# MLP weight blocks prepared a block further ahead, and DVE passes put in another order

## The chip, the cores and the metric

The kernel runs on one core of a Trainium2 chip. The metric is the device time of one execution in microseconds, the median of three runs. Five engines work beside each other, each through its own queue in order: PE (TensorE, the matmuls), DVE (VectorE) and ACT (ScalarE) for elementwise work, POOL (GpSimd) and SP (SyncE), which here mostly issue DMAs.

## What is computed

One layer of a hybrid decoder on 544 token columns (512 prompt, 32 sample tokens), in fp32:

```python
def decoder_layer(x, caches, norm_mix, w_in, ..., w_out, norm_ffn, w_up, w_down, rel_bias):
    h = rms_norm(x, norm_mix)
    z = h @ w_in                      # 2048 -> 5632: q, k, v of 3 x 4 heads, u and g of the gMLP
    ...                               # dilated window attention, and u * (W_s g + b) in chunks
    x = x + jnp.concatenate([attn, gm], axis=-1) @ w_out
    h2 = rms_norm(x, norm_ffn)
    x = x + jnp.square(jax.nn.relu(h2 @ w_up)) @ w_down      # 2048 -> 8192 -> 2048
    return x, new_kv, g
```

## The kernel before

The order on each engine is the order of the Python statements (`manual_schedule`), so what stands earlier in the code of an engine's queue holds up what stands later. The tile framework adds the semaphore waits: between SBUF accesses by the slice that they touch, for a PSUM tile by the whole tile, and for a buffer of a pool when its earlier tile is done with.

**Precision.** An fp32 factor is split into a high part (a cast to fp32r by ACT) and the remainder (a subtraction by DVE), and each product is three matmuls: high by high, high by low, low by high.

**Before the MLP.** The input projection (88 tiles), attention and gMLP come first; a planner (`Plan`) deals their small steps out between the projection's weight tiles. `gate_mix(f)` (L590) makes the four spatial gate products in the PSUM tiles `po`, `ms`, `po`, `ms`; `gate_add(f)` (L595) reads them on DVE, one planner slot later. The output projection makes 16 row tiles in pairs (`M_ORDER`); for each, `residual` (L662) adds the input on DVE, squares on ACT and stores to `x1d` from POOL's queue, and `terms(k)` (L694) makes of a pair the seven terms of the MLP's input, which `run(1)` casts to `th[k]` (ACT) and `run(2)` subtracts to `tl[k]` (DVE). `run(0)` adds the squares into `ssq`. The last pair of tiles is computed in halves: both first halves, then both second halves.

**The MLP.** It uses a seven-product scheme for 2x2 block matrices: the seven products `qs[1..7]` stand in PSUM, products 1 and 2 in one tile (`pa`), 6 and 7 in another (`pb`), 5, 4 and 3 in a tile each. There are 64 stages, 32 for `w_up` and 32 for `w_down`, of four units each; unit u = 4 s + g. A unit uses one weight block of 512 KB (`load`, from SP's queue, three slots `raw`) and is 42 matmuls in the order 1, 2, 6, 7, 5, 4, 3. For a block `prepare` (L739) does: ACT casts `vh` of the raw quarters (L751); DVE makes four opening sums `vs` (L752, two at once; L754; L755); ACT casts these (L756); DVE subtracts for `vl` (L757 from the raw quarters, L758 from the sums). `vs`, `vh` and `vl` have two buffers.

In the queues, unit u has: the fetch of block u + 3, `prepare` of block u + 1, the hooks put down for (s, g), the matmuls of unit u, and after the fourth unit `combine` (L789): ACT copies product 1 to `w` (L791), DVE forms four sums of the seven products (L792 to L798). After an up stage these are squared relu (`square`, hook at the next stage's unit 1), get the three sums of `sums` (L682; unit 2) and are stored to `rd[p]` from POOL's queue. In a down stage pair k's terms are replaced by those of the next stage: `load_terms` (L861) brings `rd` to `tl[k]`, `down_terms` (L868) casts to `th[k]` on ACT (L871) and subtracts on DVE (L872), one pair each stage, and eight pairs while up passes to down. `down_out` (L887) adds to `yd` in DRAM; the last eight stages scale and store `y` (`scaled`, L874). `start_sum` (L836) scales the residual into `yd` during the up stages, and `scale_back` (L809) makes the norm's factors in stages 2 to 4. Pair 7's terms are made by `last_terms` (L766), a hook of unit (0, 1).

## Time and profile before

| | us |
|---|---|
| median of the runs shown | 2180.43 (2175.71 to 2183.02) |
| the profiled execution | 2178.95, span 2177.2 |
| first matmul of the MLP | 765.88 |
| first matmul of its down stages | 1453.58 |
| mean granted TensorE clock | 0.988 |

The span goes from the first to the last instruction. The MLP's matmuls, 10752 of 16392, take up the last two thirds of it. Matmul records overlap (a matmul's record lasts 0.29 us, where the next starts 0.125 later), so starts tell more than lengths. An idle time in brackets behind a row is the time that the engine stood before this instruction, with the instruction whose end released it.

### The profile page before, as it was taken

Reading aid. Unit: us, or ns where it says so; the run is one execution under the profiler, and the core shown is the slowest. Engines: PE = TensorE matmul, PEld = TensorE weight load, DVE = VectorE, ACT = ScalarE, POOL = GpSimd, SP = SyncE. Lnnn points to the kernel's source line nnn. Section 1 sums busy time; section 2 is a strip of 40 time slices with the busy share of each in tenths; the row PEclk is TensorE's granted clock in tenths of the full one; section 3 lists DMA queues with packets and bytes.
Section 4 is the critical chain, followed back from the end, with each engine's and each line's share of the span. In section 5 each row is a group of like instructions: output and inputs, shape, how many; then the busy total and the mean of one; then the engine's idle time right before and its main releaser. Section 6 shows DMA issues by size and latency. Waiting matters only on the chain.

```text
span 2177.2 us, 40916 instructions
## 1 busy us (share of the span) xinstructions
PE 2091.0 (96%) x16392; PEld 2060.1 (95%) x16392; DVE 1754.4 (81%) x3566; ACT 929.3 (43%) x1296; POOL 235.4 (11%) x534
## 2 busy tenths in 40 slices
PE   8989999999889989999999999988999999999998
PEld 8989989899889989999999999988999999999998
DVE  5355767566677889989999998889888888898987
ACT  5324243342543444444444544454444444444442
POOL 3121120211211100000000000010000000000101
PEclk9999999999999999999999999999999999999999
DMA  5365655656564534445555444474565656564665
GB/s 191 99 187 174 213 200 183 205 175 206 184 190 151 181 116 133 164 157 181 170 174 178 168 162 143 151 281 151 159 179 157 182 154 181 155 182 154 217 204 156
DMA packets 109695, 378.13 MB, mean 174 GB/s; under 512 B 12640, under 2 KB 12752, under 8 KB 109504
## 3 DMA queue, kind: packets, MB, share of 16 engines
q1 hardware_dynamic: 81744, 243.58, 34.3%
q0 software_dynamic: 27760, 131.94, 19.9%
q8 instruction: 128, 2.10, 0.4%
q14 instruction: 63, 0.52, 0.1%
HBM read 305.87 MB, written 69.21 MB: 172 GB/s over the span
## 4 chain that ended last, share of the span: by engine, by line
PE 46%; issue 33%; DMA 9%; DVE 7%; POOL 2%; ACT 2%; POOLq 0%; SPq 0%; DVEq 0%; ACTq 0%
PE pt L87 13%; PE pt L931 6%; PE pt L933 6%; PE pt L932 6%; DMA kv<-in_kc_dram 3%; PE sm L931 2%; PE sm L932 2%; PE po L931 2%; PE po L932 2%; PE sm L933 2%; PE ms L931 2%; PE ms L933 2%; PE po L933 2%; PE ms L932 2%; DMA kv<-in_vc_dram 1%
## 5 line engine op out<-in xcount | busy, mean ns | idle before, releaser
L931 PE MATMUL pt<-th,vh 128*128 128x272 f32 x2048 | 597.9, 292 | 23.7 <-DVE o L792 16.6
L932 PE MATMUL pt<-tl,vh 128*128 128x272 f32 x2048 | 594.7, 290 | 7.3 <-DVE tl L872 7.3
L933 PE MATMUL pt<-th,vl 128*128 128x272 f32 x2048 | 594.0, 290 | 3.8 <-DVE vl L757 3.8
L756 ACT CAST vh<-vs 128x1024 fp32r<-128x1024 f32 x256 | 269.4, 1052 | 405.4 <-DVE vs L755 403.9
L931 PEld LDWEIGHTS pt<-th,vh 128*128 128x128 f32 x2048 | 388.6, 190 | 30.8 <-DVE o L792 20.7
L932 PEld LDWEIGHTS pt<-tl,vh 128*128 128x128 f32 x2048 | 389.3, 190 | 8.4 <-DVE tl L872 8.4
L933 PEld LDWEIGHTS pt<-th,vl 128*128 128x128 f32 x2048 | 389.7, 190 | 4.2 <-DVE vl L757 4.2
L751 ACT CAST vh<-raw 128x768 fp32r<-128x768 f32 x256 | 213.5, 834 | 339.3 <-PE po L932 202.8
L758 DVE TENSOR_TENSOR vl<-vs,vh 128x1024 fp32r<-128x1024 f32 x256 | 313.8, 1226 | 54.3 <-ACT vh L756 53.7
L87 PE MATMUL pt<-hh,wh 128*128 128x272 f32 x1408 | 302.8, 297 | 6.0 <-DVE wh L78 6.0
L87 PE MATMUL pt<-hl,wh 128*128 128x272 f32 x1408 | 294.5, 291 | 0.5 <-DVE hl L183 0.5
L87 PE MATMUL pt<-hh,wl 128*128 128x272 f32 x1408 | 294.5, 291 | 0.0
L757 DVE TENSOR_TENSOR vl<-raw,vh 128x768 fp32r<-128x768 f32 x256 | 244.0, 953 | 19.3 <-ACT vh L751 17.6
L87 PEld LDWEIGHTS pt<-hh,wh 128*128 128x128 f32 x1408 | 224.1, 192 | 17.0 <-ACT hh L182 6.0
L79 DVE TENSOR_TENSOR wl<-raw,wh 128x512 fp32r<-128x512 f32 x208 | 145.3, 700 | 108.0 <-ACT wh L78 107.0
L87 PEld LDWEIGHTS pt<-hl,wh 128*128 128x128 f32 x1408 | 225.0, 192 | 0.9 <-DVE hl L183 0.9
L87 PEld LDWEIGHTS pt<-hh,wl 128*128 128x128 f32 x1408 | 223.8, 192 | 0.0
L78 ACT CAST wh<-raw 128x512 fp32r<-128x512 f32 x200 | 121.5, 615 | 151.3 <-PE pt L87 137.2
L752 DVE TENSOR_TENSOR vs<-raw 128x512 f32<-128x512 f32 x256 | 175.1, 684 | 0.0
L931 PE MATMUL po<-th,vh 128*128 128x272 f32 x512 | 147.8, 289 | 0.0
L931 PE MATMUL sm<-th,vh 128*128 128x272 f32 x512 | 147.5, 288 | 0.0
L933 PE MATMUL po<-th,vl 128*128 128x272 f32 x512 | 147.5, 288 | 0.0
(233 smaller groups left out, 3768.5 us busy)
## 6 DMA issues: line engine op xcount, KB each, us to landing
raw<-in_w_up_dram SPq DMA_DIRECT2D x128, 512.0 KB
raw<-in_w_down_dram SPq DMA_DIRECT2D x128, 512.0 KB
raw<-in_w_in_dram SPq DMA_DIRECT2D x84, 512.0 KB
tl<-rd POOLq DMA_DIRECT2D x39, 952.0 KB, 7.7
rd<-f POOLq DMA_DIRECT2D x32, 952.0 KB, 4.4
kv<-in_kc_dram SPq DMA_DIRECT2D x96, 256.0 KB
kv<-in_vc_dram SPq DMA_DIRECT2D x96, 256.0 KB
yd<-o POOLq DMA_DIRECT2D x39, 544.0 KB, 5.5
```

What stands on the lines that cost most here:

```text
L78: copy(wh, r)
L79: V.tensor_tensor(wl, r, wh.bitcast(F32), op=OP.subtract)
L87: mm(pt[:, c, :NH], wt[:, j, :], at[:, c * NH:(c + 1) * NH], start=start and n == 0, stop=stop and n == 2)
L751: A.copy(vh[:, :3 * VB], raw[:, VB:])
L752: V.tensor_tensor(pair(vs[:, :2 * VB]), raw[:, None, :VB].to_broadcast([P, 2, VB]), pair(raw[:, VB:3 * VB]), op=OP.add)
L756: A.copy(vh[:, 3 * VB:], vs)
L757: V.tensor_tensor(vl[:, :3 * VB], raw[:, VB:], vh[:, :3 * VB].bitcast(F32), op=OP.subtract)
L758: V.tensor_tensor(vl[:, 3 * VB:], vs, vh[:, 3 * VB:].bitcast(F32), op=OP.subtract)
L931: mm(qs[n], vh[:, c], th[k][:, t, :], start=first, stop=False)
L932: mm(qs[n], vh[:, c], tl[k][:, t, :], start=False, stop=False)
L933: mm(qs[n], vl[:, c], th[k][:, t, :], start=False, stop=last)
```

## The change

- `prepare` is cut in two. `sum_weights` makes the opening sums, now two blocks ahead: L752 and L754 ahead of the split of the next block, L755 behind it. `split_weights` does both casts (ACT) and both subtractions (DVE), one block ahead.
- `combine` uses three slices of one tile `w` (one buffer; two before) and another order of its sums.
- Where output projection and MLP meet, block 0 is summed and split ahead of the last two residuals, and block 1 summed behind them. What `run(2)` and `run(0)` do for pair 6 and the last squares moves to hooks of units (0, 0) and (0, 1).
- The three sums after an up stage go to units 2, 3 and 0 of the next stages, the store to `rd` with the last one. `start_sum`'s scaling goes from unit 3 to unit 1. From the ninth pair on `down_terms` goes from unit 2 or 3 of the load's stage to unit 1 of the next one.
- Gate products 2 and 3 go to tiles of the small PSUM ring (two buffers) instead of `po` and `ms`.

The matmuls, their order, the loads and the arithmetic stay.

```diff
     def gate_mix(f):
-        po = gates[f]["po"] = ps.tile([P, 512], F32, name=("po", "ms")[f % 2])
+        po = gates[f]["po"] = ps.tile([P, 512], F32, name=("po", "ms")[f]) if f < 2 else small_psum()
...
     def sums(f):
         V.tensor_tensor(f[:, 0:2, :], f[:, 7:8, :].to_broadcast([P, 2, NH]), f[:, 4:7:2, :], op=OP.subtract)
+        yield
         V.tensor_tensor(f[:, 2, :], f[:, 6, :], f[:, 0, :], op=OP.subtract)
+        yield
         V.tensor_tensor(f[:, 3, :], f[:, 5, :], f[:, 2, :], op=OP.subtract)
...
-    run(0)
+    pts = [main_psum() for _ in range(2)]
+    for part in range(2):
+        for pt in pts:
+            half(pt, part)
     mix.close()
...
-        A.copy(vh[:, :3 * VB], raw[:, VB:])
+    def sum_weights(u):
+        raw = raws[u]
+        vs = summed[u] = uw.tile([P, 4 * VB], F32, name="vs", tag=f"vs{u % 2}")
         V.tensor_tensor(pair(vs[:, :2 * VB]), raw[:, None, :VB].to_broadcast([P, 2, VB]), pair(raw[:, VB:3 * VB]),
                         op=OP.add)
         V.tensor_tensor(part(vs, 2), part(vs, 1), part(raw, 1), op=OP.add)
+        yield
         V.tensor_tensor(part(vs, 3), part(vs, 2), part(raw, 3), op=OP.add)
+        yield
+
+    def split_weights(u):
+        raw, vs = raws[u], summed[u]
+        vh, vl = (uw.tile([P, 7 * VB], F32R, name=n, tag=f"{n}{u % 2}") for n in ("vh", "vl"))
+        A.copy(vh[:, :3 * VB], raw[:, VB:])
         A.copy(vh[:, 3 * VB:], vs)
         V.tensor_tensor(vl[:, :3 * VB], raw[:, VB:], vh[:, :3 * VB].bitcast(F32), op=OP.subtract)
         V.tensor_tensor(vl[:, 3 * VB:], vs, vh[:, 3 * VB:].bitcast(F32), op=OP.subtract)
...
     for i in range(3):
-        fetch(units[i])
-    ready = [prepare()]
+        fetch(i)
+    list(sum_weights(0))
+    split_weights(0)
+    for m, pt in zip(M_ORDER[KD - 2:], pts):
+        residual(m, pt)
+    list(sum_weights(1))
 
     def last_terms():
         nonlocal yp
+        run(0)
...
     def combine(c11, c12, c21, c22):
-        w = uw.tile([P, NH], F32, name="w", bufs=2)
-        A.copy(w, qs[1])
-        V.tensor_tensor(c11, qs[2], w, op=OP.add)
-        V.tensor_tensor(w, qs[6], w, op=OP.subtract)
-        V.tensor_tensor(c21, qs[7], w, op=OP.add)
-        V.tensor_tensor(w, qs[5], w, op=OP.add)
-        V.tensor_tensor(c22, qs[5], c21, op=OP.add)
-        V.tensor_tensor(c21, qs[4], c21, op=OP.add)
-        V.tensor_tensor(c12, qs[3], w, op=OP.subtract)
+        w = uw.tile([P, 3, NH], F32, name="w")
+        w1, w2, w3, x = (w[:, i, :] for i in (0, 1, 0, 2))
+        A.copy(w1, qs[1])
+        V.tensor_tensor(w2, qs[6], w1, op=OP.subtract)
+        V.tensor_tensor(c11, qs[2], w1, op=OP.add)
+        V.tensor_tensor(x, qs[7], w2, op=OP.add)
+        V.tensor_tensor(w3, qs[5], w2, op=OP.add)
+        V.tensor_tensor(c22, qs[5], x, op=OP.add)
+        V.tensor_tensor(c21, qs[4], x, op=OP.add)
+        V.tensor_tensor(c12, qs[3], w3, op=OP.subtract)
...
+    hook(0, 0, run, 2)
     hook(0, 1, last_terms)
...
-        hook(8 + 2 * q, 3, rest)
+        hook(8 + 2 * q, 1, rest)
...
+        parts = sums(f)
+        hook(p + 1, 1, square)
+        hook(p + 1, 2, partial(next, parts))
+        hook(p + 1, 3, partial(next, parts))
+
+        def last():
+            next(parts, None)
             G.dma_start(out=rd[p], in_=f[:, :7, :])
 
-        hook(p + 1, 1, square)
-        hook(p + 1, 2, rest)
+        hook(p + 2, 0, last)
...
-                                ((first, 0), (first, 2)), ((first, 0), (first, 2)), ((first, 1), (first, 3)))):
+                                ((first, 0), (first, 2)), ((first, 0), (first, 2)), ((first, 1), (first + 1, 1)))):
...
         hook(UPG + t, 1, load_terms, t + PAIRS)
-        hook(UPG + t, 2, down_terms, t + PAIRS)
+        hook(UPG + t + 1, 1, down_terms, t + PAIRS)
...
-        if u + 3 < len(units):
-            fetch(units[u + 3])
+        fetch(u + 3)
+        sums_next = sum_weights(u + 2) if u + 2 < len(units) else iter(())
+        next(sums_next, None)
         if u + 1 < len(units):
-            ready.append(prepare())
+            split_weights(u + 1)
+        next(sums_next, None)
         for fn in hooks.get((s, g), []):
             fn()
```

## Rows read from the trace of the kernel before

**Rows 1.** The page: busy us of each engine, share of the span, instructions.
```profile
PE 2091.0 (96%) x16392; PEld 2060.1 (95%) x16392; DVE 1754.4 (81%) x3566; ACT 929.3 (43%) x1296; POOL 235.4 (11%) x534
```

**Rows 2.** Stretches of the MLP: length, PE, PEld, DVE, ACT, POOL busy, PEclk, DMA.
```profile
765.88:793.34 27.46, 23.38 (x168) 22.72 (x168) 23.38 (x32) 10.60 (x12) 0.00 (x0) 0.94 0.29 89
793.34:923.00 129.66, 128.09 (x1013) 127.04 (x1013) 119.00 (x192) 58.79 (x67) 5.77 (x10) 1.00 0.46 152
923.00:1429.40 506.40, 506.40 (x4035) 506.40 (x4033) 457.49 (x729) 235.86 (x264) 21.24 (x40) 1.00 0.49 164
1453.58:1490.34 36.76, 27.51 (x168) 26.00 (x168) 33.24 (x37) 21.39 (x18) 1.06 (x2) 0.86 0.54 211
1490.34:2145.28 654.94, 640.19 (x5040) 635.12 (x5041) 580.75 (x846) 285.28 (x299) 49.26 (x71) 1.00 0.59 176
```

**Rows 3.** Who PE waited for in the MLP: us in total, times, longest us.
```profile
PE pt L931 <- DVE o L792: 16.6, 17, 2.0
```

**Rows 4.** DVE in one down stage, in time: start us, us, instruction, idle before.
```profile
1641.01 0.44 DVE L792 TENSOR_TENSOR o<-pt,w 128x272 f32<-128x272 f32 x1
1641.55 0.44 DVE L793 TENSOR_TENSOR w<-pt,w 128x272 f32<-128x272 f32 x1
...
1644.17 0.68 DVE L752 TENSOR_TENSOR vs<-raw 128x512 f32<-128x512 f32 x1
1644.89 0.43 DVE L754 TENSOR_TENSOR vs<-vs,raw 128x256 f32<-128x256 f32 x1
1645.35 0.43 DVE L755 TENSOR_TENSOR vs<-vs,raw 128x256 f32<-128x256 f32 x1
1645.69 0.95 DVE L757 TENSOR_TENSOR vl<-raw,vh 128x768 fp32r<-128x768 f32 x1
1646.89 1.23 DVE L758 TENSOR_TENSOR vl<-vs,vh 128x1024 fp32r<-128x1024 f32 x1 [0.25 <-ACT vh L756]
1648.03 0.69 DVE L752 TENSOR_TENSOR vs<-raw 128x512 f32<-128x512 f32 x1
...
1656.78 2.14 DVE L872 TENSOR_TENSOR tl<-tl,th 128x1904 fp32r<-128x1904 f32 x1 [0.92 <-ACT th L871]
...
1662.70 0.43 DVE L792 TENSOR_TENSOR o<-pt,w 128x272 f32<-128x272 f32 x1
```

**Rows 5.** DVE in the last stage, in time.
```profile
2155.37 1.28 DVE L876 TENSOR_TENSOR o<-o,rb 128x1088 f32<-128x1088 f32 x1
```

**Rows 6.** DVE where up passes to down, first and last of 36 rows.
```profile
1448.99 4.19 DVE L872 TENSOR_TENSOR tl<-tl,th 128x1904 fp32r<-128x1904 f32 x2 [0.46 <-ACT th L871]
...
1489.86 0.43 DVE L792 TENSOR_TENSOR o<-pt,w 128x272 f32<-128x272 f32 x1
```

**Rows 7.** PE in the MLP's first stage, in time: its first matmul and one of block 3.
```profile
765.88 0.39 PE L931 MATMUL pt<-th,vh 128*128 128x272 f32 x1 [2.28 <-ACT vh L751]
...
787.76 0.39 PE L933 MATMUL pt<-th,vl 128*128 128x272 f32 x1 [1.85 <-DVE vl L757]
```

**Rows 8.** DVE at the same place, in time.
```profile
763.64 0.72 DVE L664 TENSOR_TENSOR x<-pt,x 128x544 f32<-128x544 f32 x1 [0.24 <-PE pt L87]
...
775.94 0.96 DVE L757 TENSOR_TENSOR vl<-raw,vh 128x768 fp32r<-128x768 f32 x1 [0.84 <-ACT vh L751]
...
783.08 2.14 DVE L691 TENSOR_TENSOR tl<-f,th 128x1904 fp32r<-128x1904 f32 x1 [1.85 <-ACT th L691]
```

**Rows 9.** PE at the third gate product and the second output tile, in time.
```profile
653.42 2.05 PE L593 MATMUL po<-gwt,gt 128*128 128x128 f32 x8 [3.65 <-DVE z L598]
...
667.33 0.77 PE L87 MATMUL pt<-cat,wh 128*128 128x272 f32 x4
```

**Rows 10.** DVE between these two: the read of the last input tile.
```profile
663.83 0.72 DVE L630 TENSOR_TENSOR z<-pt,rb 128x544 f32<-128x544 f32 x1
```

**Rows 11.** The page: a group (busy us, mean ns, idle before) and a DMA issue.
```profile
L752 DVE TENSOR_TENSOR vs<-raw 128x512 f32<-128x512 f32 x256 | 175.1, 684 | 0.0
...
tl<-rd POOLq DMA_DIRECT2D x39, 952.0 KB, 7.7
```

More of the change, by code (lines that the diff above doesn't have):

```diff
@@ L2 @@
 from functools import partial
-from itertools import cycle, islice
+from itertools import islice
 import numpy as np
@@ L697, in terms @@
             V.scalar_tensor_tensor(dst, halves(x1[m]), gn[:, 16 + m:17 + m], halves(rb), op0=OP.mult, op1=OP.mult)
-        sums(f)
+        list(sums(f))
         after[1].append(partial(A.copy, th[k], f[:, :7, :]))
@@ L709, in half @@
         run(part)
-    for i, m in enumerate(M_ORDER):
-        if 2 <= i < KD - 2:
+    for i, m in enumerate(M_ORDER[:KD - 2]):
+        if i >= 2:
             pts = [main_psum()]
@@ L715, in hybrid_layer_kernel @@
                 half(pts[0], part)
-        elif i == KD - 2:
-            pts = [main_psum() for _ in range(2)]
-            for part in range(2):
-                for pt in pts:
-                    half(pt, part)
         residual(m, pts.pop(0))
@@ L724, in hybrid_layer_kernel, with fetch, part, pair @@
             after[0].append(first_scale)
-        for k in {3: [0], 4: [1]}.get(i, [i // 2] if i % 2 and 4 < i < KD - 1 else []):
+        for k in {3: [0], 4: [1]}.get(i, [i // 2] if i % 2 and i > 4 else []):
             terms(k)
-        if i + 2 < KD:
-            x_load(M_ORDER[i + 2])
-    run(0)
+        x_load(M_ORDER[i + 2])
+    pts = [main_psum() for _ in range(2)]
+    for part in range(2):
+        for pt in pts:
+            half(pt, part)
     mix.close()
     uw = ctx.enter_context(tc.tile_pool(name="uw", bufs=1, side="right", reuse_waits="tile"))
-    turns = cycle(range(2))
-    raws = []
-    def fetch(src):
-        raws.append(load(src))
-    def prepare():
-        raw = raws.pop(0).rearrange("p a b -> p (a b)")
-        n = next(turns)
-        vs = uw.tile([P, 4 * VB], F32, name="vs", tag=f"vs{n}")
-        vh, vl = (uw.tile([P, 7 * VB], F32R, name=v, tag=f"{v}{n}") for v in ("vh", "vl"))
-        def part(t, i):
-            return t[:, i * VB:(i + 1) * VB]
-        def pair(t):
-            return t.rearrange("p (a b) -> p a b", a=2)
-        A.copy(vh[:, :3 * VB], raw[:, VB:])
+    raws, summed, ready = {}, {}, {}
+    def fetch(u):
+        if u < len(units):
+            raws[u] = load(units[u]).rearrange("p a b -> p (a b)")
+    def part(t, i):
+        return t[:, i * VB:(i + 1) * VB]
+    def pair(t):
+        return t.rearrange("p (a b) -> p a b", a=2)
+    def sum_weights(u):
+        raw = raws[u]
+        vs = summed[u] = uw.tile([P, 4 * VB], F32, name="vs", tag=f"vs{u % 2}")
         V.tensor_tensor(pair(vs[:, :2 * VB]), raw[:, None, :VB].to_broadcast([P, 2, VB]), pair(raw[:, VB:3 * VB]),
@@ L852, in square @@
             A.activation(f[:, 4:, :], f[:, 4:, :], AF.Square)
-        def rest():
-            sums(f)
+        parts = sums(f)
[4 more added lines that the diff above has]
+            next(parts, None)
             G.dma_start(out=rd[p], in_=f[:, :7, :])
-        hook(p + 1, 1, square)
-        hook(p + 1, 2, rest)
+        hook(p + 2, 0, last)
     def load_terms(n):
```

4 lines of the change are left out of this document (2 added, 2 removed).

## Prediction

> **What bounds the kernel now.** I read the page first: TensorE (PE) is busy 96% of the span, VectorE (DVE) 81% [rows 1]. That does not say what a microsecond taken from DVE is worth, so the next view cuts the MLP into stretches [rows 2]. A stage is 168 matmuls. In the third stretch 24 stages take 506.40 us, or 21.10 each, with PE busy throughout: no stage can be shorter. Against that floor the other stretches lose:
>
> - the first stage 27.46 - 21.10 = 6.4 (and 2.3 before its first matmul);
> - the next six 129.66 - 126.6 = 3.1;
> - the last up stage, from 1429.40 to 1453.58, 3.1, and the first down stage 36.76 - 21.10 = 15.7, together 18.7;
> - the 30 down stages from 1490.34, 654.94 - 633.0 = 21.9.
>
> These 52 us are all that work on the MLP can win. The third view is who ends PE's waits: in the down stages it is L792, the first DVE instruction of `combine`, 17 times [rows 3]. The first matmul of a stage writes a PSUM tile that L792 has to have read. The fourth view tells why L792 is late [rows 4]: in this down stage DVE stands still only for ScalarE (ACT), and from L792 to the next L792 is 1662.70 - 1641.01 = 21.69 us, longer than PE's 21.10. So DVE sets the pace there, as it does in the first stage and where up passes to down; in between PE does.
>
> **The change part by part.**
>
> *One weight block on DVE.* Before, from L752 to the next L752 is 1648.03 - 1644.17 = 3.86 [rows 4]: starts 0.72, 0.46, 0.34, 1.20 and 1.14 apart. Two parts of that go. L755 reads what L754 has just written, and starts 0.46 after it; an instruction that touches nothing of its predecessor's starts 0.34 after one of that size (L755 to L757). I count 0.35. With L755 behind L758 this saves 0.11. L758 stands 0.25 for ACT's cast of the sums; once the sums lie a block ahead that cast follows the first one at once, so 1.20 becomes 0.95. The pair L752, L754 stays together, 0.72. New block: 0.72 + 0.35 + 0.95 + 1.14 + 0.35 = 3.51, saving 0.35.
>
> *`combine`.* Before 1644.17 - 1641.01 = 3.16 for seven instructions, of which one that overwrites its predecessor's operand starts 0.54 behind it (L792 to L793) [rows 4]. In the new order neighbours share no slice: 7 x 0.35 = 2.45, saving 0.71. Against it, the tile that the next stage's first matmul writes is now read by the second instruction, not the first: 0.35 later, which counts only where DVE is late.
>
> *Down stages.* DVE needs 21.69 - 4 x 0.35 - 0.71 = 19.6, and 18.7 if the 0.92 that L872 stands for ACT goes too (its cast moves a stage later, so the load behind it has landed long before). Both are under 21.10. In unit 3 DVE waits for PE to free the `vl` slot, then needs about 0.95 + 0.95 + 1.14 + 0.35 + 0.70 = 4.1 up to the PSUM release, where PE takes 5.27 (a quarter of 21.10); what is late next is PE itself. Of 21.9 I take 21.3. The lower bound: were only the stand at L758 to go, 4 x 0.25 = 1.0, a stage would need 20.7; the eight last ones with L876 on top, 1.28 [rows 5], would need 22.0 and lose 0.9 each, 7.2 together. So 14.7 to 21.9.
>
> *Up to down.* DVE works from 1448.99 to L792 at 1489.86 almost without a stop, 40.9 us [rows 6]. It loses three block savings (1.1), one `combine` saving less the 0.35 above (0.4), three stands like the 0.46 before L872, whose cast was queued behind ACT's wait for sums (1.4), and the ninth L872 with its stand, which moves a stage later (2.06 + 0.46 = 2.5), where DVE has 1.5 spare; about 0.4 is moved out with the split of the opening sums. Sum 5.8; PE follows DVE here. Bounds 3.0 (the stands stay and the last sums fall before a `combine`) and 8 (one half-clock spell less: PE was granted 0.86 over these 36.76, so 10 us ran at half speed, three spells costing 1.7 each [rows 2]).
>
> *Start of the MLP.* Before, PE waits 2.28 for the first cast and later 1.85 at block 3, whose low half L757 is late [rows 7]. The first block's sums and split now stand ahead of the last residuals, on ACT and DVE alike, and the two residuals (L664, ACT's square, POOL's store each) behind them. The blocks' loads come from SP's queue, which nothing moved here passes. By the sizes in the code the first block's space overlaps only operands that the output projection uses in its first halves, so its 3.5 us fit beside PE's last 6 us of products, and PE can go on without a stop. But block 3 then decides, as before. From L664 of the last residual, 763.64, to L757 of block 3 [rows 8] the queue loses block 0 (3.86), a stand at block 2 (0.84) and three savings (1.05), and gains the subtraction of pair 6 (2.1, as the L691 in [rows 8]) and the opening sums of block 4 (0.72 + 0.35): 2.6 sooner. PE, idle longer in one piece, should then run another spell at half clock; the window's 0.94 over 27.46 says that the one before was 3.3 us long and cost 1.65 [rows 2]. I take 1.5: most of the 8.7 lost here is moved, not won. Bounds: 3.2 without that spell; -1.2 if the first block must wait for the last product after all, since the residuals then wait behind it, and so do the PSUM tiles that PE needs.
>
> *Next six stages.* Of 3.1, I take 1.0: `square` and the second reciprocal no longer make L792 late, but the first reciprocal now does, because the opening sum and the new second place of the PSUM read follow it. Bounds -1 and 2.4.
>
> *Gate products.* PE waits 3.65 for the addition that frees the PSUM tile [rows 9]; in other tiles it needn't wait. DVE is busy without a break there, and reads the last input tile at 663.83 [rows 10]; the second output tile cannot start before 664.6, where it started at 667.33 [rows 9], and its operands come from the same DVE queue. So at most 2.7, I take 2.0, at least 0.
>
> *The rest at nothing.* The `rd` stores go two units later on POOL's queue, 11% busy [rows 1], and are read many stages later, the last one 22. `yd`'s scaling goes from unit 3 to unit 1, clear of `combine`, two units after its load. `w` has one buffer instead of two and is free a stage before its next use. Uncovered, none is over 1 us once. The end of the kernel: 0.2.
>
> *Sum.* 21.3 + 5.8 + 1.5 + 1.0 + 2.0 + 0.2 = 31.8, between 15.5 and 38.5. The profiled execution took 2178.95 us (span 2177.2), 1.5 below the median of 2180.43; the sum comes off either. Prediction 2180.43 - 31.8 = 2148.6.
>
> **The rivals.**
>
> *Neighbours cost the same whatever they touch.* Then 0.11 a block and 0.71 a `combine` stay. Down stages give 14.7, up to down 5.1 (0.3 and 0.4 less), start 1.2, the rest 2.5: 23.5, so 2156.9. For it: every pair in question also differs in what it waits for. Against it: the 0.46 and the 0.34 stand between instructions of one size in one block [rows 4]. This is also how the Trainium skill has it ("VectorE: DVE Perf Modes", section "The DRAIN you can't avoid"): the next operation waits until the pipe is empty, and chaining operations without semaphores saves nothing. The rows differ from that. Chance 0.12.
>
> *A new wait in place of the old.* DVE now stands at L757 for PE in every unit, and `combine` in unit 3 has 5.27 - 4.1 = 1.1 us to spare. If ACT's two casts, now back to back, come 1.5 later than I count, each down stage loses 0.4 again: 12 in 30, so 2161. For it: ACT also carries L871 and `combine`'s copy. Against it: ACT is busy 43% [rows 1]. Chance 0.08.
>
> *Slower: three load slots.* Opening sums read a block one unit sooner, and its load can't start until L757 of three blocks before has read the slot. Two blocks on DVE then take a load plus 0.72 + 0.35 + 0.95 = 2.0 us; that exceeds two units of PE, 10.5, once issue to landing takes over 8.5 us. At 9.7 us every block would take 5.85, 0.58 too much: 256 x 0.58 = 148 less what is won, some 2300. Against it: L752 never stood for a load [rows 11], and the nearest row, a 952 KB transfer (a block is 512 KB), lands after 7.7. Chance 0.03, another 0.02 for anything else that ends slower.
>
> **How the numbers follow.** Forecast 0.70, first rival 0.12, second 0.08, slower 0.05 (0.01 of it by too little to tell), 0.03 that the down stages stay as they are and the rest gives under 6 us, 0.02 for a gain beyond the bounds. The bounds give 2141.9 and 2164.9; the runs before spread by some 5 us, so the range is 2140 to 2166, which takes in the first two rivals. This kernel's measurement tells 0.3% (6.5 us) from no change: faster 0.92, same 0.04, slower 0.04.
>
> **What would show it.** Right: down stages of 21.1 to 21.2 with no wait on the instructions of `combine`; L758 not standing for ACT; `combine` from first to last in about 2.5; the stretch after 1453 some 6 shorter; PE waiting for L757 of block 3 in one long piece; no wait at the third gate product. Wrong: `combine` still at 3.1 (first rival); DVE idle behind ACT's casts in unit 3 while PE waits (second); L752 standing for a load (third); PE's first MLP matmul later than before, which sinks the term for the start.

## The result: 2146.7 us, and where the 31 us came from

| | before | changed |
|---|---|---|
| median of the runs beside each other, us | 2181.72 (2174.38 to 2183.62) | 2146.73 (2144.22 to 2148.22) |
| profiled execution, us | 2178.95, span 2177.2 | 2148.09, span 2146.3 |
| mean granted TensorE clock | 0.988 | 0.987 |

The ratio of the times is 0.9846, with a 95% interval of 0.9827 to 0.9864; the forecast was 2148.6. The medians lie 35.0 us apart and the two profiled executions 30.9, since the one before was 2.8 under its median and the changed one 1.4 over. Of all executions below one is left out as disturbed, of the kernel without the weights part: it took 4081.54 us at a granted clock of 1.0. The page of the changed kernel shows what [rows 1] showed, with 55 us less on VectorE (DVE):

```profile
PE 2080.3 (97%) x16392; PEld 2055.3 (96%) x16392; DVE 1699.6 (79%) x3566; ACT 908.1 (42%) x1296; POOL 236.1 (11%) x534
```

The stretches of the MLP, cut as in [rows 2] (stage 0; 1 to 6; 7 to 30; 31; 32; 33 to 62), each with its length, the busy time of PE, PEld, DVE, ACT and POOL, the granted clock, the DMA share and GB/s:

```profile
764.83:793.99 29.16, 23.82 (x170) 23.38 (x169) 26.20 (x39) 9.86 (x11) 0.55 (x1) 0.88 0.26 83
793.99:922.43 128.44, 127.43 (x1015) 126.47 (x1013) 111.08 (x187) 57.78 (x67) 5.27 (x9) 1.00 0.43 143
922.43:1426.75 504.32, 504.32 (x4035) 504.32 (x4034) 436.07 (x729) 229.50 (x264) 21.31 (x40) 1.00 0.49 165
1426.75:1453.57 26.82, 21.18 (x171) 20.99 (x169) 21.17 (x31) 17.96 (x17) 4.75 (x9) 0.94 0.84 327
1453.57:1483.26 29.69, 25.64 (x169) 24.55 (x169) 29.55 (x37) 14.67 (x14) 1.06 (x2) 0.88 0.56 205
1483.26:2114.17 630.91, 630.91 (x5041) 630.91 (x5042) 559.40 (x850) 273.13 (x300) 50.02 (x72) 1.00 0.62 185
```

In the last of them PE is busy for all of the 630.91 us, where it was busy for 640.19 of 654.94: the 30 down stages are 24.0 us shorter and wait for nothing. DVE needs 559.40 / 30 = 18.65 us a stage there. Who ends PE's waits in the MLP, as in [rows 3]:

```profile
PE pt L946 <- DVE f L801: 5.6, 1, 5.6
PE pt L947 <- DVE tl L885: 3.9, 4, 1.4
PE pt L946 <- ACT vh L757: 3.4, 2, 2.5
PE pt L948 <- DVE vl L759: 2.9, 1, 2.9
```

The 17 waits for the first DVE instruction of `combine` are gone; what is left lies at the start and where up passes to down. In time, a piece of a down stage on DVE, to be laid beside [rows 4] (L747, L749, L751 are the opening sums, L759 and L760 the split, L800 to L806 `combine`):

```profile
1626.27 0.96 DVE L759 TENSOR_TENSOR vl<-raw,vh 128x768 fp32r<-128x768 f32 x1 [1.25 <-ACT vh L757]
1627.22 1.23 DVE L760 TENSOR_TENSOR vl<-vs,vh 128x1024 fp32r<-128x1024 f32 x1
1628.36 0.42 DVE L751 TENSOR_TENSOR vs<-vs,raw 128x256 f32<-128x256 f32 x1
1628.70 0.43 DVE L800 TENSOR_TENSOR w<-pt,w 128x272 f32<-128x272 f32 x1
1629.05 0.43 DVE L801 TENSOR_TENSOR o<-pt,w 128x272 f32<-128x272 f32 x1
...
1631.14 0.68 DVE L747 TENSOR_TENSOR vs<-raw 128x512 f32<-128x512 f32 x1
```

`combine` takes 1631.14 - 1628.70 = 2.44 us, where it took 3.16; its instructions start 0.35 apart. The split's second half no longer stands for its cast. DVE now stands 1.25 us for a cast that itself waits for PE to leave the slot (ACT starts it at 1625.40, and the unit's first matmul is at 1625.03): it has time to spare.

Between the two profiled executions 30.9 us of span went. By starts of matmuls:

| piece | before | changed | won | forecast |
|---|---|---|---|---|
| up to the 4500th matmul (untouched code) | 614.4 | 617.0 | -2.6 | 0 |
| from there to the last matmul of the output projection | 148.9 | 147.8 | 1.2 | 2.0 |
| gap to the MLP and stage 0 | 30.0 | 29.3 | 0.75 | 1.5 |
| stages 1 to 6 | 129.7 | 128.4 | 1.2 | 1.0 |
| stages 7 to 30 | 506.4 | 504.3 | 2.1 | 0 |
| stages 31 and 32 | 60.9 | 56.5 | 4.4 | 5.8 |
| stages 33 to 62 | 654.9 | 630.9 | 24.0 | 21.3 |
| stage 63 and the end | 31.9 | 32.2 | -0.3 | 0.2 |

Two rows were not foreseen: 24 stages in which PE never waited got shorter, and code that nobody touched took 2.6 us longer. The experiments ask which part won the down stages, what shortened a stage without waits, and what the start, the gates and the way from up to down are worth.

### The profile page after: what moved, and what is told of

Same layout as the page of the kernel before. It is cut to its first block, busy times and chain, and to the rows that moved or that the text cites. A ratio compares the mean times of both kernels' runs of the same rounds, so it can differ in the third digit from the quotient of the medians.

```text
span 2146.3 us, 41107 instructions
## 1 busy us (share of the span) xinstructions
PE 2080.3 (97%) x16392; PEld 2055.3 (96%) x16392; DVE 1699.6 (79%) x3566; ACT 908.1 (42%) x1296; POOL 236.1 (11%) x534
## 4 chain that ended last, share of the span: by engine, by line
PE 73%; issue 10%; DMA 8%; DVE 7%; ACT 1%; POOL 1%; SPq 0%; POOLq 0%; DVEq 0%; ACTq 0%
PE pt L946 12%; PE pt L948 12%; PE pt L947 12%; PE pt L87 12%; DMA kv<-in_kc_dram 4%; PE sm L947 3%; PE sm L948 3%; PE sm L946 3%; PE ms L948 3%; PE po L948 3%; PE ms L946 3%; PE po L947 3%; PE ms L947 3%; PE po L946 3%; DMA fb<-fr 2%
## 5 line engine op out<-in xcount | busy, mean ns | idle before, releaser
L759 DVE TENSOR_TENSOR vl<-raw,vh 128x768 fp32r<-128x768 f32 x256 | 244.7, 956 | 144.2 <-ACT vh L757 143.8
L760 DVE TENSOR_TENSOR vl<-vs,vh 128x1024 fp32r<-128x1024 f32 x256 | 313.0, 1223 | 0.3 <-ACT vh L758 0.3
L758 ACT CAST vh<-vs 128x1024 fp32r<-128x1024 f32 x256 | 268.3, 1048 | 3.5 <-DVE vs L751 3.4
L747 DVE TENSOR_TENSOR vs<-raw 128x512 f32<-128x512 f32 x256 | 175.1, 684 | 7.4 <-DMA raw<-in_w_down_dram 7.2
L948 PE MATMUL ms<-th,vl 128*128 128x272 f32 x512 | 147.5, 288 | 0.0
L946 PE MATMUL ms<-th,vh 128*128 128x272 f32 x512 | 147.4, 288 | 0.0
L947 PE MATMUL sm<-tl,vh 128*128 128x272 f32 x512 | 147.3, 288 | 0.0
```

The costliest lines, as they stand in the source:

```text
L747: V.tensor_tensor(pair(vs[:, :2 * VB]), raw[:, None, :VB].to_broadcast([P, 2, VB]), pair(raw[:, VB:3 * VB]), op=OP.add)
L758: A.copy(vh[:, 3 * VB:], vs)
L759: V.tensor_tensor(vl[:, :3 * VB], raw[:, VB:], vh[:, :3 * VB].bitcast(F32), op=OP.subtract)
L760: V.tensor_tensor(vl[:, 3 * VB:], vs, vh[:, 3 * VB:].bitcast(F32), op=OP.subtract)
L946: mm(qs[n], vh[:, c], th[k][:, t, :], start=first, stop=False)
L947: mm(qs[n], vh[:, c], tl[k][:, t, :], start=False, stop=False)
```

## Experiments: one part alone

**The weights part alone.** In the kernel before, the opening sums go two blocks ahead, split and sums as in the change; `combine`, `down_terms`, the gates and the order at the start (residuals first) stay. Of the edit, the end of the loop:

```diff
...
         if u + 1 < len(units):
-            ready.append(prepare())
+            split_weights(u + 1)
+        next(sums_next, None)
```

> The kernel before with one part of the change alone: opening sums two blocks ahead, split one block ahead (at the start too, but behind the last residuals). Forecast theory (a down stage is as long as the slower of PE and DVE): DVE falls by 4 x 0.35 from 21.69 to 20.3 us, below PE's 21.1, so most down stages go to PE's floor by this part alone; the last eight, where DVE has 1.28 more, stay at 21.6; 30 down stages 633 to 638 us instead of 654.94, the time 2160 to 2164 us against 2180. Neighbours cost the same: 20.7 and 22.0, 640 us. Rival (each part is worth its share of the DVE time saved, 1.4 of 3.0): 11 of the 24 us, 644 us. On the floor: if the order of the weights' passes lowers it, the stages 7 to 30 take 21.01 each instead of 21.10.

Measured: 2161.54 us (ratio 0.9921, 0.9899 to 0.9942); the 30 down stages 647.95 us, so 7.0 won in the profiled execution and not 17 to 22; stages 7 to 30 506.40; stages 31 and 32 56.73 (4.2 won). The last eight stages are at 21.0 to 21.1, but stages between them take up to 24.5. Who ends DVE's waits in the down stages:

```profile
DVE vs L748 <- DMA raw<-in_w_down_dram: 27.3, 24, 4.2
DVE tl L877 <- ACT th L876: 22.1, 20, 4.6
DVE vl L760 <- ACT vh L758: 15.0, 17, 1.7
```

and one such place in time, on ACT and then on DVE:

```profile
1741.14 1.78 ACT L876 CAST th<-tl 128x1904 fp32r<-128x1904 f32 x1 [4.35 <-DMA tl<-rd]
```

```profile
1742.96 2.14 DVE L877 TENSOR_TENSOR tl<-tl,th 128x1904 fp32r<-128x1904 f32 x1 [4.57 <-ACT th L876]
```

The load of `tl` is issued in unit 1 and cast in unit 2. Relieved of 1.4 us, DVE and ACT come there before the load has landed (median 7.7 us behind its issue, at most 11.5), stand up to 4.6, and what stood behind them is late; opening sums that read a block one unit sooner then find that block still on its way, 24 times. A wait behind a load took the place of the wait that was removed.

How much that costs varies from execution to execution. The profiled one is the slowest of four, 2168.52 us at a granted clock of 0.984; the others took 2159.35 to 2163.29 at 0.986 to 0.988. In the 15.0 us that its 30 down stages take over the floor, PE's waits are 8.4 (from 1490 us on):

```profile
PE pt L938 <- DVE o L797: 8.4, 6, 3.3
```

The rest is mostly half clock: PE was granted 0.50 from 1490.0 to 1491.8, from 1747.8 to 1754.6 and from 1986.8 to 1990.2, 12 us together, which costs up to 6. So the 647.95 miss the forecast of 633 to 638, but the median time lies inside the forecast's 2160 to 2164. It is 18.1 under the median before; with 4.2 won in stages 31 and 32 and 1.2 in stages 1 to 6, some 12 to 13 us are left for the down stages of a usual execution (an estimate), which is nearer to the rival's 11 than to the forecast.

**The new `combine` alone.**

```diff
-        V.tensor_tensor(c11, qs[2], w, op=OP.add)
-        V.tensor_tensor(w, qs[6], w, op=OP.subtract)
+        V.tensor_tensor(w2, qs[6], w1, op=OP.subtract)
+        V.tensor_tensor(c11, qs[2], w1, op=OP.add)
```

> The kernel before with the new combine alone. Forecast theory (a down stage is as long as the slower of PE and DVE; shared slices cost time): DVE falls by 0.71 from 21.69 to 20.98 us, just below PE's 21.1; the last eight stages need 22.3; the 30 down stages take 633 + 8 x 1.2 = 642 us, at most 647 as the margin is thin and the PSUM tile is released 0.35 later, instead of 654.94. Combine 2.45 instead of 3.16. Neighbours cost the same: 655 us, no change. Each part worth its share (0.71 of 3.0): 649 us. On the floor: if combine lowers it, the stages 7 to 30 take 21.01 each, else 21.10.

Measured: 2168.57 us (0.9944, 0.9927 to 0.996); the 30 down stages 647.16, 7.8 won, at the end of what the first theory allows (at most 647). Of stages 7 to 30 some took 21.01 and some 21.10 or a little more; what holds the second kind is not settled.

**The later `down_terms` alone.**

```diff
-        hook(UPG + t, 2, down_terms, t + PAIRS)
+        hook(UPG + t + 1, 1, down_terms, t + PAIRS)
```

> The kernel before with the later down_terms alone (from the ninth pair on, in unit 1 of the next stage). Forecast theory (a down stage is as long as the slower of PE and DVE): the 0.92 us that the subtraction of tl stands for its cast goes, DVE falls from 21.69 to 20.8 us; the last eight stages need 22.05; the 30 down stages take 633 + 8 x 0.95 = 641 us instead of 654.94. Stages 31 and 32 together 2.5 shorter (the ninth pair's subtraction leaves them): 58.4 instead of 60.95. If the stand does not go because the cast stands behind others of ACT in unit 1 too: 30 down stages 650 to 655. Each part worth its share (0.92 of 3.0): 648 us. On the floor: the stages 7 to 30 have no down_terms, so they stay at 21.10.

Measured: 2169.19 us (0.9954, 0.9938 to 0.9969); the 30 down stages 642.14, most of them 21.2 and the last of them 22.4, as expected; stages 31 and 32 58.93 (2.0 won), stages 7 to 30 506.40. Stage 63 and the end took 34.8 us in this execution, where they took 31.9 before; why is open.

Alone, the three win 7.0, 7.8 and 12.8 us of the down stages in these single executions, 27.6 together, where the whole change wins 24.0 and the floor allows no more. By the medians of whole executions they win 18.1, 11.1 and 10.5, where the whole change wins 35.0. Either way the parts add up to more than the whole, but which part is worth most alone is not settled. A stage is as long as the slower engine, so what a part is worth depends on the others.

## Experiments: one part undone

**`combine` as before.** The changed kernel with the old function.

> The changed kernel with the old combine (one w, two buffers, neighbours that share slices, PSUM read first). Forecast theory (a down stage is as long as the slower of PE and DVE; shared slices cost DVE time): combine from its first to its last DVE instruction 3.16 again instead of 2.44; DVE then needs 18.7 + 0.7 = 19.4 us a down stage, still under PE's 21.0, so the 30 down stages stay at 21.0 to 21.1 each (631 to 634 us together, 630.91 changed) and the time at 2146 to 2150 us. Up to down: the two DVE instructions there lose 0.7 and gain 0.35, stages 31 and 32 together 56.5 to 57.5 (56.51 changed). Rival (DVE time saved is worth its length wherever it is saved): 30 x 0.7 = 21 us slower, 2168. Rival (neighbours cost the same): combine 2.44 to 2.5, nothing changes. On the floor: PE's stage without waits was 21.10 us before and is 21.01 changed; if the combine's reads of PSUM lower it, the stages 7 to 30 go back to 21.10 each.

Measured: 2149.51 us (0.9863, 0.9848 to 0.9877); the 30 down stages 632.15, stages 31 and 32 57.24. Two instructions of the old function, and the one behind it:

```profile
1629.45 0.43 DVE L799 TENSOR_TENSOR o<-pt,w 128x272 f32<-128x272 f32 x1
1629.99 0.44 DVE L800 TENSOR_TENSOR w<-pt,w 128x272 f32<-128x272 f32 x1
...
1632.61 0.68 DVE L747 TENSOR_TENSOR vs<-raw 128x512 f32<-128x512 f32 x1
```

It takes 3.16 us again, with 0.54 where an instruction overwrites an operand of its predecessor. So neighbours don't cost the same whatever they touch. With the rest in place the 0.7 us are worth next to nothing in a down stage: 1.2 in 30, with most stages between 21.03 and 21.10. Stages 7 to 30 are back at 506.40: whatever made PE's own stage shorter came with the new `combine`, and it can account for the 1.2 as well.

**The weights part undone.** The opening sums stand with their split again, one block ahead.

```diff
-        sums_next = sum_weights(u + 2) if u + 2 < len(units) else iter(())
-        next(sums_next, None)
         if u + 1 < len(units):
             split_weights(u + 1)
-        next(sums_next, None)
```

> The changed kernel without its weights part: a block's opening sums stand with its split again, one block ahead. Forecast theory (a stage is as long as the slower of PE and DVE): DVE needs 18.7 + 1.4 = 20.1 us a down stage, the last eight 21.4; the 30 down stages take 631 to 636 us (630.91 changed). Stages 31 and 32: three blocks at 0.35 dearer, but the wait of 3.4 us for a weight block that the changed kernel has in stage 31 goes, as the block is read a unit later: 54 to 57 us (56.51 changed). The time 2146 to 2153. Rival (the weights part carries the gain, 1.4 of 3.0 us of DVE time): 11 us more in the down stages, 2158.

Measured: 2150.05 us (0.9869, 0.9853 to 0.9886); the 30 down stages 633.38, the last of them 21.7; stages 31 and 32 57.88, 0.9 above what was expected, although the wait for a weight block is gone there.

**`down_terms` back in the unit behind its load.**

> The changed kernel with down_terms back in the unit behind its load (unit 2 of the same stage, the ninth in unit 3 of stage 32). With the old combine, or with the old weights part, the 30 down stages stayed at PE's floor (632.15 and 633.38 us); with the weights part alone they took 647.95, where the subtraction of tl stood 22 us for its cast and the opening sums 27 us for weight blocks. Theory A (the pace of DVE decides: 18.7 + 0.92 = 19.6 us a stage): 631 to 633 us, the time 2147 to 2151. Theory B (with the opening sums two blocks ahead, DVE and ACT run up to PE and then stand for the load of tl, which lands too late for unit 2, and the blocks' loads come late behind it): 640 to 650 us, 2156 to 2166 us. In both, stages 31 and 32 2 to 2.5 longer by the ninth pair's subtraction, 58.5 to 59.

Measured: 2157.16 us (2151.42 to 2159.35; 0.9903, 0.9884 to 0.9921). In the profiled execution, whose span of 2149.6 us is the shortest of four, the 30 down stages take 638.73, most of them at 21.0 and some up to 23.9; stages 31 and 32 58.58. DVE's waits in the down stages:

```profile
DVE vl L759 <- ACT vh L757: 53.0, 59, 1.7
DVE tl L885 <- ACT th L884: 10.8, 8, 3.1
DVE vs L747 <- DMA raw<-in_w_down_dram: 8.8, 14, 1.6
```

It is the second theory's mechanism: the same stands as with the weights part alone are back. Its price in this execution, 7.8 us, is under the 9 to 19 that the theory gave, while the median of the four lies inside its 2156 to 2166. Of the three parts this is the one that can't be left out: undone, `combine` costs 1.2 us in the down stages, the weights part 2.5, this one 7.8; and the medians are 2149.51, 2150.05 and 2157.16, beside 2146.73 for the whole change.

## Experiments: what shortened a stage without waits

**Only the place of a buffer.** In the kernel before, `w` gets the size that it has in the changed one. No instruction changes and none moves.

```diff
-        w = uw.tile([P, NH], F32, name="w", bufs=2)
+        w = uw.tile([P, 3, NH], F32, name="w")[:, 0, :]
```

> The kernel before with nothing but the place of a buffer changed: w is one tile of three slices of which the first is used (3264 bytes in a partition), where it was two buffers of one slice (2176). Instructions and their order are the same. The stage without waits was 21.10 us before and with the weights or the down_terms part alone, 21.01 with the new combine. Theory (PE's pace hangs on where the operands lie in SBUF): the 24 stages 7 to 30 take 504.3 us instead of 506.4. Theory (it hangs on the order in which PSUM is read): 506.4. Otherwise as before: 30 down stages 650 to 655 us, 2177 to 2181 us in all.

Measured: 2178.88 us (1.0005, 0.9996 to 1.0015), 30 down stages 652.13, and for stages 7 to 30:

```profile
925.19:1429.51 504.32, 504.32 (x4035) 504.32 (x4034) 456.88 (x729) 236.04 (x264) 21.25 (x40) 1.00 0.49 165
```

That is the 504.32 of the changed kernel to the digit, beside 506.40 in [rows 2]. The bigger `w` takes 1088 bytes more in each partition, so tiles of its pool, which holds the weights' tiles and the last pair's terms, lie elsewhere in SBUF. Where tiles lie thus changes PE's pace, by 0.5 ns a matmul (125.1 against 125.6 from start to start). Whether it is the place of what PE itself reads, or of what the other engines read and write meanwhile, no run separates. And place is not all: the new `combine` alone has the same `w`, and stages of both kinds.

## Experiments: start, gates, and the way from up to down

**Residuals first.** The changed kernel with block 0 behind the last residuals again.

```diff
-    list(sum_weights(0))
-    split_weights(0)
     for m, pt in zip(M_ORDER[KD - 2:], pts):
         residual(m, pt)
+    list(sum_weights(0))
+    split_weights(0)
```

> The changed kernel with one thing undone: the two last residuals stand ahead of block 0's sums and split again. Forecast theory (block 3's split decides when PE can go on, and the same work stands ahead of it in DVE's queue in both orders): the gap before the first MLP matmul comes back, 2.3 to 2.5 us, and stage 0 gets shorter by nearly as much; gap and stage 0 together 28 to 30 us (29.16 changed, 29.91 before), the time within 1.5 us of the changed kernel's 2147. Rival (the gap is won outright): 31.5 us together, 2149 to 2150. Rival (slower clock after the longer stand of PE in one piece costs what the missing gap gives): gap and stage 0 together 27 to 28 us.

Measured: 2149.08 us (0.9866, 0.9852 to 0.9881); the gap of 2.4 is back (2.6 from start to start of PE's matmuls) and stage 0 takes 29.74, 32.3 together against 29.3. That is the rival's number. The expectation had a slip: it called the work ahead of block 3 the same in both orders, but behind the last residual there is one block more, 3.86 us by [rows 4], as the prediction had counted. So the move of block 0 is worth 3.0, and what else the change did here takes 2.3 of it back (30.0 before). The subtraction of pair 6 and the squares, which it put into stage 0, are the likely cause; alone they were not run.

**Gate products 2 and 3 back in `po` and `ms`.**

```diff
-        po = gates[f]["po"] = ps.tile([P, 512], F32, name=("po", "ms")[f]) if f < 2 else small_psum()
+        po = gates[f]["po"] = ps.tile([P, 512], F32, name=("po", "ms")[f % 2])
```

> The changed kernel with gate products 2 and 3 back in the tiles po and ms. Forecast theory (PE waits there for the addition that frees the tile, and the wait was 3.65 us before): the wait of the third gate product on the addition comes back, 3 to 4 us, and the stretch from PE's matmuls around 629 us to those around 720 us is 2.0 us longer than in the changed kernel (between 0 and 2.7); the MLP is unchanged; time 2147 to 2150 us. Rival (DVE sets the end of that stretch whatever PE waits for): the wait comes back and the stretch stays as long, to 0.5 us.

Measured: 2148.1 us (0.9858, 0.9837 to 0.9879). PE's wait is back, as in [rows 9]:

```profile
PE po L593 <- DVE z L598: 2.6, 1, 2.6
```

In the changed kernel the longest wait between 610 and 685 us is another one, for a weight half:

```profile
PE pt L87 <- DVE wl L79: 1.9, 1, 1.9
```

Since all these kernels have either the old or the new gate tiles and the rest of this stretch alike, its length can be read from 14 executions (starts of PE's matmuls by their number, us):

| matmuls | old tiles, mean of 6 | new tiles, mean of 8 |
|---|---|---|
| 4620 to 4860 (gates, last input tiles) | 34.5 | 30.9 |
| 4860 to 5000 (first output tiles) | 18.3 | 21.8 |
| 4500 to 5000 | 67.5 (66.7 to 67.9) | 67.4 (66.9 to 68.4) |

The 3.6 us are won at the gate and given back within 140 matmuls. How, seven of the eight executions with new tiles show (not the changed kernel's own); in the one without the weights part PE stands at the second output tile until DVE has read the last input tile,

```profile
PE pt L87 <- DVE z L630: 1.7, 1, 1.7
```

and then runs a spell at half clock (the stretch after that wait, columns as above):

```profile
665.50:670.20 4.70, 4.64 (x25) 4.67 (x26) 3.25 (x7) 2.46 (x5) 0.00 (x0) 0.64 0.10 10
```

1.7 us of waiting and 0.36 x 4.70 = 1.7 of clock make up 3.4 of the 3.8 that this execution gives back (22.1 in the second row). The rival's half of the expectation holds: the term is 0.

**DVE's work on POOL.** The changed kernel, relieved in the stretches where DVE is still the bound: pair 6's subtraction and the last squares' additions on POOL, also the subtractions of three pairs where up passes to down; opening sums behind split and hooks there; the scale steps of stages 2 to 4 a unit earlier. Of the edit, the part where up passes to down:

```diff
...
+        E = G if n in (3, 5, 7) else V
         A.copy(th[k], raw)
-        V.tensor_tensor(tl[k], raw, th[k].bitcast(F32), op=OP.subtract)
+        E.tensor_tensor(tl[k], raw, th[k].bitcast(F32), op=OP.subtract)
```

> The changed kernel with DVE relieved in the three stretches where it is still the bound. Start: the last squares' additions and pair 6's subtraction on POOL, opening sums behind the split and the hooks in stage 0, pair 7's subtraction behind block 3's sums. Up to down: the subtractions of pairs 3, 5 and 7 on POOL, opening sums behind split and hooks in stages 31 and 32. Stages 2 to 4: the scale steps a unit earlier. Forecast theory (PE follows DVE in these stretches): DVE loses 1.5 + 2.1 + 1.8 in stage 0, which ends 4 us sooner (25 us); 6.2 of 50.9 us in stages 31 and 32 and the wait of 3.4 for a block beside combine, together 48 to 52 us instead of 56.5; stages 1 to 6 127.3 instead of 128.4. Time 2133 to 2140 us. Rival (POOL's subtraction of 1904 columns, 5.4 us by the 1.55 of an addition of 544, is late for PE or slows DVE beside it): stages 31 and 32 55 us or more, DVE's instructions longer than 1.22 and 2.14 there, 2142 to 2150.

Measured: 2152.95 us (0.9883, 0.9868 to 0.9898). Gap and stage 0 take 27.9 and stages 1 to 6 127.26, but stages 31 and 32 64.5, 8 more than in the changed kernel. POOL, then DVE, at the first such subtraction, and DVE at a later one:

```profile
759.01 4.48 POOL L703 TENSOR_TENSOR tl<-f,th 128x1904 fp32r<-128x1904 f32 x1 [3.70 <-ACT th L694]
```

```profile
759.38 4.39 DVE L752 TENSOR_TENSOR vs<-vs,raw 128x256 f32<-128x256 f32 x1
...
1467.20 4.70 DVE L748 TENSOR_TENSOR vs<-raw 128x512 f32<-128x512 f32 x1
```

A sum that takes 0.42 us takes 4.39 beside POOL's subtraction of 4.48. DVE does not slow down beside POOL, it stands: 4.5 us on POOL cost DVE more than the 2.1 that the subtraction takes there. The Trainium skill says so ("SBUF — State Buffer", section "SBUF: two separate sides"): the two share a pair of ports, and whichever of a POOL instruction that reads SBUF and a DVE instruction with two SBUF inputs comes first holds it for its whole length. The trace agrees, with 4.39 against 0.42.

DVE's stands are one part of the loss. In the other PE stands for POOL's own subtraction, which is done later than DVE's would be (in the changed kernel PE's waits for `tl` are 3.9 us in all, on DVE):

```profile
PE pt L963 <- POOL tl L891: 8.1, 3, 3.4
```

Both parts of the rival hold: POOL is late for PE, and DVE stands beside it.

**Another order, nothing on POOL.** The changed kernel with the same aims by order alone: pair 6's subtraction between the two last residuals, where DVE stood for PE; opening sums behind split and hooks in stages 0, 31 and 32; the last squares two units later; the sums of the last two up stages after the transition; the casts of `down_terms` there a unit earlier; the scale steps a unit earlier. Two places of the edit:

```diff
...
     for m, pt in zip(M_ORDER[KD - 2:], pts):
         residual(m, pt)
+        run(2)
...
-            hook(2 + n // 2, 2 + n % 2, fn)
+            hook(2 + n // 2, 1 + n % 2, fn)
```

> The changed kernel with DVE's queue put in another order in the three stretches where DVE still sets the pace, nothing on POOL. Start: pair 6's subtraction between the two last residuals, where DVE stood 2.3 us; opening sums behind split and hooks in stage 0; pair 7's subtraction behind block 3's sums; the last squares' additions two units later. Stages 2 to 4: the scale steps a unit earlier. Up to down: the sums of the last two up stages (2.8 us) after the transition, their stores with them, the casts to th a unit earlier, opening sums behind split and hooks, in unit (31, 3) behind combine. Forecast theory (DVE sets the pace there and every microsecond taken out of its queue counts once): gap and stage 0 together 24 to 26 us (29.16 changed), stages 1 to 6 127.0 to 127.6 (128.4), stages 31 and 32 together 52 to 54.5 (56.5), the rest as changed; time 2135 to 2141 us. Rival (the loads of tl set the pace in the transition: eight of 952 KB land one behind the other in 24 us): stages 31 and 32 stay at 56, time 2140 to 2143.

Measured: 2138.36 us (2138.14 to 2139.59), ratio to before 0.9812, 0.9794 to 0.983: the fastest of all. Stage 0 and the two transition stages:

```profile
760.92:784.45 23.53, 21.45 (x171) 21.04 (x169) 22.17 (x32) 10.80 (x12) 0.55 (x1) 1.00 0.27 85
1422.80:1480.38 57.58, 46.84 (x338) 45.37 (x337) 50.70 (x65) 30.78 (x29) 5.13 (x9) 0.94 0.65 232
```

Stage 0 is 5.6 us shorter than in the changed kernel, without a gap ahead of it, and its granted clock is 1.00 where it was 0.88: with PE's long waits the spell at half clock went too. Which of the moves at the start won how much is not separated. Stages 1 to 6 take 127.18. Stages 31 and 32 take 57.58, 1.1 more, not the 52 to 54.5 expected. DVE is busy there for the same 50.7 us as in the changed kernel (21.17 + 29.55 in the windows above), and has 6.9 us of waits in place of 5.8: ACT's casts, put ahead of the weights' casts, held these up while `tl` was landing:

```profile
DVE vl L759 <- ACT vh L757: 6.5, 4, 3.6
```

The rival, that the loads of `tl` set the pace there, is nearer to the number.

**The same, 32 bytes further.** The operands of the MLP's matmuls begin at multiples of 64 bytes.

```diff
+    tp.tile([P, 8], F32, name="pad")
...
-        w = uw.tile([P, 3, NH], F32, name="w")
+        w = uw.tile([P, 3 * NH + 8], F32, name="w")
```

> The same kernel with the operands of the MLP's matmuls 32 bytes further in SBUF (a pad ahead of th, a w of 8 more columns), so that they begin at multiples of 64 bytes. Instructions and order are the same. Theory (only the place counts, and of places only the distance between the operands of one matmul): stages 7 to 30 21.01 each as before the pad, or back at 21.10. Theory (a start that is a multiple of 64 bytes is cheaper to read): under 21.01 each, every 0.1 us being 6 us in all. If it is dearer, over 21.1. Otherwise stage by stage as the run without the pad.

Measured: 2143.87 us (0.9837, 0.9818 to 0.9856), stages 7 to 30 506.40 again:

```profile
915.50:1421.90 506.40, 506.40 (x4035) 506.40 (x4034) 436.00 (x729) 229.47 (x264) 21.27 (x40) 1.00 0.49 164
```

So a start at a multiple of 64 bytes is not what makes the cheaper place. Which relation of the operands does is open.

## Why the prediction was right, and where it wasn't

*What bounds it.* Right. The term of the down stages, 21.3 forecast, came as 24.0: all that they lost against the floor of [rows 2], 21.9, and 2.1 more because the floor itself fell from 21.10 to 21.03. That floor is the one thing said there that was wrong: "no stage can be shorter" than 21.10, where the place of a tile alone made it 21.01. DVE's need was counted as 18.7 and is 18.65. Its steps hold one by one: L760 stands 0.3 us for its cast in all where L758 stood 53.7, `combine` takes 2.44 (2.45 forecast), the subtraction of `tl` stands no more. "What is late next is PE itself" is what the windows show.

*One step in that argument was missing, without harm.* The prediction gave `down_terms` a worth of 0.92 us a stage and treated the three savings as one sum. The kernels with a part left out show that the later `down_terms` is what lets the other two count: faster DVE queues run into the load of `tl` unless the cast moves behind it (without it 7.8 us of the down stages are lost again, and with the weights part alone DVE stands 22.1 us for the casts of `tl` and 27.3 for blocks). The second rival, a new wait in place of the old, named the casts; in the whole change it did not come, in the partial one it came behind a load.

*Neighbours.* The first rival fell: 3.16 with the old order and 2.44 with the new, in kernels that are otherwise alike. The Trainium skill's rule that the prediction weighed ("VectorE: DVE Perf Modes", section "The DRAIN you can't avoid") has an exception in the same section, which the prediction left out: a next operation that is not held starts earlier. The trace agrees with the exception: these 272-column instructions last 0.43 and start 0.35 apart. Still, the 0.7 us were worth at most 1.2 us in 30 stages, since the bound had already gone over to PE.

*Up to down.* 5.8 forecast, 4.4 measured. The term that failed is the one that left the loads out. DVE in stage 31:

```profile
1444.77 0.69 DVE L747 TENSOR_TENSOR vs<-raw 128x512 f32<-128x512 f32 x1 [3.44 <-DMA raw<-in_w_down_dram]
...
1448.18 4.19 DVE L885 TENSOR_TENSOR tl<-tl,th 128x1904 fp32r<-128x1904 f32 x2
```

and what PE made of it:

```profile
1453.57 0.56 PE L946 MATMUL pt<-th,vh 128*128 128x272 f32 x1 [5.64 <-DVE f L801]
```

While the eight loads of `tl` pass, an opening sum, which now reads its block a unit sooner, stands 3.44 us for it. This is the third rival's mechanism, at one place that PE felt; four more such stands in the down stages, 3.8 us in all, cost it nothing. With the sums a block later the wait is gone, but the two stages take 57.88: the weights part still wins there, by less than it was given. The clock helped, which the forecast had put into its upper bound alone: stage 32 ran at 0.88, which costs up to 3.6 us, where it ran at 0.86 and lost up to 5.1 before. The 0.94 of stage 31 cost nothing, since the half clock there fell into PE's wait of 5.64. So without some 1.5 of clock the terms of the sum gave about 2.9 of their 5.8 (an estimate), and the stand of 3.44 is of the size of what is missing.

*Start.* 1.5 forecast, 0.75 measured, by the mechanism forecast. Against the last matmul of the output projection, the one that waits for block 3's low half comes 786.60 - 764.71 = 21.9 us later, before 787.76 - 763.31 = 24.5 [rows 7]: 2.6 sooner, which is the sum that the prediction made. Behind that matmul the stage took 793.99 - 786.60 = 7.39, before 793.34 - 787.76 = 5.58: 1.8 of the 2.6 went again, at a granted clock of 0.66, where the forecast had counted 1.65 for such a spell. What the forecast has too much is in the 3.2 that it gives without the spell, from which the 1.5 follows: its own sum is 2.6, and for the other 0.6 it gives no reason. PE's two waits, which the prediction expected in one piece:

```profile
783.23 0.39 PE L946 MATMUL pt<-th,vh 128*128 128x272 f32 x1 [2.48 <-ACT vh L757]
786.60 0.59 PE L948 MATMUL pt<-th,vl 128*128 128x272 f32 x1 [2.86 <-DVE vl L759]
```

"Most of the 8.7 lost here is moved, not won" was true of this change, not of the place: another order of the same work wins 5.6 us there.

*Stages 1 to 6.* 1.0 forecast, 1.2 measured; scale steps a unit earlier win another 1.2, half of the 2.4 that was left over the floor of 6 x 21.01. The weights part alone wins the 1.2 too (128.42), and without it they stay (128.26): here, too, the parts do not add up.

*Gates.* 2.0 forecast, 0 measured. (The 1.2 in the table lies in the spread: over the 14 executions that stretch took 147.9 to 148.9 with the old gate tiles and 147.5 to 149.1 with the new ones.) The prediction saw that the second output tile can't start before DVE has read the last input tile [rows 10], and put its bound there, at 2.7. The failing step is what comes behind that bound: it counted no price for PE standing there, and the wait of 1.7 at L630 with the spell at half clock behind it take the gain back. In the start's term it had counted such a spell; here it didn't. In the changed kernel's own profile the wait and a spell (granted 0.83 from 629.9 to 640.0) come at a weight half instead, ahead of the gates; why there in that execution is open.

*What made up for it.* The floor gave 4.2 us that no term held (2.1 in stages 7 to 30, 2.1 in the down stages). The gates (by the mean of the 14 executions), the transition and the start fell short by 2.0 + 1.4 + 0.75 = 4.2. That the sum came out within 1 us of the span's 30.9, in spite of 2.6 lost in the front of this one execution, is partly chance; the medians' 35.0 is 3.2 over the sum. That front is code nobody touched, and the time of its 4500th matmul runs from 611.2 to 617.0 us over 14 executions, with the changed kernel's among the latest, so a single profile can't tell 3 us of its own.

## What to carry to other kernels

Where two engines take turns as the bound, find the floor first and count savings as "under the floor or not", not as a sum: here either of two savings could be left out at little cost, and the third, a cast moved further behind its load, was the one that they needed. A wait that PE shows is worth its length only if no later wait on the same engine follows; measure the stretch up to a point that both kernels reach, not the wait. And look for stands of the bounding engine that other work in its own queue could fill: that was worth more here than moving work to an engine that shares its ports.

## What the runs showed of the hardware

- PE's pace without waits hangs on where tiles lie in SBUF: 125.1 or 125.6 ns from start to start of a 128x272 matmul, 21.01 or 21.10 us a stage, with identical instructions. In the changed kernel's down stages, whose terms move from pair to pair, all but the first (21.16) take 21.01 to 21.05, and the same lengths come back every eight stages, the number of pairs.
- A subtraction of 1904 columns takes 2.14 us on DVE and 4.48 to 6.06 on POOL, and a DVE instruction with two SBUF inputs that starts beside it lasts until POOL is done (4.39, 4.48, 4.70 and 4.78 us instead of 0.42 to 0.72).
- In the changed kernel a load of 952 KB lands 7.1 us behind its issue in the median, and 11.2 where eight of them followed each other; a 512 KB load on another queue was 3.4 us late for its reader beside them.
